# Encoder block on one Trainium2 core: five conv input pairs as Strassen products among the gate pairs, depthwise taps of four blocks on ScalarE and GpSimd

## The chip, the cores and the metric

One core of a Trainium2 chip runs the whole kernel in one launch. The metric is device time in microseconds. TensorE (PE) multiplies matrices, VectorE (DVE), ScalarE (ACT) and GpSimd (POOL) work on tiles, SyncE (SP) issues most of the loads. SBUF is the memory on the chip, PSUM the accumulators of TensorE.

## The reference

One residual layer over 512 tokens of 2048 features in float32. Cut to what this change touches:

```python
u = rms_norm(h, mix_pre_g)
proj = u @ w_in          # q, k, v, conv_a, conv_b (1024 each), gate_attn, gate_conv (2048 each)
y_attn = neighbourhood_attention(q, k, v, rpb) @ w_attn_o
z = ca * sigmoid(cb)                       # GLU
z = depthwise_conv(z, w_dw, width 31) + b_dw   # along the 512 tokens, each channel by itself
y_conv = silu(layer_norm(z)) @ w_conv_o
merged = sigmoid(ga) * y_attn + sigmoid(gb) * y_conv
h = h + rms_norm(merged @ w_out)
h = h + rms_norm((silu(gate) * up) @ w_down)   # gate, up = rms_norm(h) @ w_gate_up
```

## The kernel before

Features lie on the 128 partitions, the 512 tokens along a row, so that each output tile is 128x512. Float32 products are made of two halves: a weight tile is cast to `hi` on ACT (fp32r) and `lo = w - hi` is made on DVE; the activations are split likewise. A plain product is hi*lo + hi*hi + lo*hi, three matmuls of 512 columns for each of 16 blocks of 128 features (`gemm`, L178; `wchunk`, L137, loads, casts and subtracts one chunk of 8 blocks).

A pair of output blocks can instead be made by one Strassen product (Winograd's form) of 2x2 blocks (`strassen`, L264): seven products of 8 blocks each, where each block takes one matmul of 512 columns with the high half of the weights and one of 256 columns with the low half. Its moving operands (`op`, 56 tiles) are differences of parts of the normalised input. Each Strassen has seven casts of 128x1024 weights on ACT and seven subtractions on DVE (`halved_weights`, L250), three sums of weights on DVE (`wsum`, L274; the lines named by the profile are those of the calls and of L276 and L332), a weight sum S1 made by an accumulating DMA that POOL issues (`sums`, L237), three additions on DVE of a PSUM product and a copied tile (L317, L324, L330), and four joins of 256 columns (`joined`, L342).

The order of the work in the part that the change touches:

1. Input: the pairs 0 and 1 of conv_a and conv_b together with the load of x, with inputs that aren't yet normalised; their outputs are multiplied by the row factor `r1` in `conv`.
2. Plain conv pairs 2 to 7 (L493): for each, `gemm` of `cb` and of `ca`, then `conv` (L420), which makes z = ca * sigmoid(cb), starts the tile `cv` with the middle tap and the bias, and puts the other 30 taps on the list `todo`. During the last pair two chunks of x are loaded again and normalised (`normalize`, L484).
3. V (L504) in two halves, with the normalisation of the other chunks in the first.
4. Q, K and the attention, head by head (L596).
5. The first two gate pairs plainly, beside the making of the Strassen operands (L633).
6. Gate pairs 2 to 15 by Strassen (L692), each output through a sigmoid on ACT and stored to `g_d`. The layer norm's sum over channels (`csum`) is multiplied by ones behind the last one.
7. The attention's output product, the conv's layer norm and output product, the output projection, and the SwiGLU part, which is again mostly Strassen products.

The taps are DVE instructions `a += w * z` on shifted rows (`taps`, L440, instruction at L446). Every `wchunk` issues `rate` of them from the list: 4 a chunk in the conv stage, 3 and 4 in the halves of V, 4 in Q and K. `tc.keep_in_program_order` pins an instruction to its place in the program; the rest is put in order on each engine by a planner from its own costs and priorities. `issued_behind` (L102) only orders, it makes no engine wait.

On the memory: 66 slots of 128x512 hold most tiles; 56 of them are the Strassen operands in the gate stage. PSUM has eight banks in two pools, from which Strassens take three tiles in turn.

Of the kernel before, what the change touches and what calls it, by code (L numbers as in the profile page):

```python
# [31 lines left out]
P = 128  # L32
# [27 lines left out]
LN_AT = 5  # L60
R_CONV, R_V, R_QK = 4, (3, 4), 4
TAIL = 200
# [13 lines left out]
def hybrid_block(ctx: ExitStack, tc, xT, vecs, rpb, mask, w_c0, w_qk, w_v, w_gg, w_cg, w_ao, w_co, w_out, w_g0, w_gu, w_dn, outT):  # L76
# [54 lines left out]

    todo, rate = [], 0

# [130 lines left out]
    def strassen(w0, w1, op, name, n, s1=None, behind_last=None, first=None, quarters=None, apart=False, turn=True, midway=None):  # L264
# [19 lines left out]
        def product(ps, w, b, first=False, last=False, lo_first=False):  # L284
            hi, lo = w if isinstance(w, tuple) else halved_weights(w, name)
            ws = [slice(k * P, (k + 1) * P) for k in range(HT)]
            steps = [(hi, slice(0, NT)), (lo, A)]
            if lo_first:
                steps.reverse()
            for n, (wt, cols) in enumerate(steps):  # L290
                for k, t in enumerate(op[b]):
                    nc.tensor.matmul(
                        ps[:, cols], wt[:, ws[k]], t[:, cols], start=first and n + k == 0,
                        stop=last and n + k == HT, skip_group_check=True,
                    )

        def done(ps, i):
# [122 lines left out]
    def conv(i, pa, pb):  # L420
        sg = slot(f"sg{i}")
        nc.vector.tensor_tensor(out=sg, in0=pb, in1=r1, op=ALU.mult)
        nc.scalar.activation(sg, sg, AF.Sigmoid)
        nc.gpsimd.tensor_tensor(out=sg, in0=sg, in1=r1, op=ALU.mult)
        z = slot(f"z{i}")
        nc.vector.tensor_tensor(
            out=z.rearrange("p (r b c) -> p b r c", r=ROWS, b=2 * NB),
            in0=pa.rearrange("p (b r c) -> p b r c", r=ROWS, b=2 * NB),
            in1=sg.rearrange("p (b r c) -> p b r c", r=ROWS, b=2 * NB),
            op=ALU.mult,  # L430
        )
        a = slot(f"cv{i}")
        nc.vector.tensor_scalar(
            out=a, in0=z, scalar1=col(C_WDW, i * CW + PAD), scalar2=col(C_BDW, i), op0=ALU.mult, op1=ALU.add
        )
        for w in range(CW):
            if w != PAD:
                todo.append((i, z, a, w))

    def taps(n):  # L440

        for i, z, a, w in todo[:n]:
            to = slice(max(0, PAD - w), NT - max(0, w - PAD))
            fr = slice(max(0, w - PAD), NT - max(0, PAD - w))
            tc.keep_in_program_order(
# [4 lines left out]
            if w == CW - 1:  # L450
                if i == 0:
                    nc.gpsimd.tensor_copy(csum, a)
                else:
                    nc.gpsimd.tensor_tensor(out=csum, in0=csum, in1=a, op=ALU.add)  # L454
                nc.gpsimd.dma_start(c_d[i], a)
        del todo[:n]
# [35 lines left out]
    rate = R_CONV  # L492
    for i in range(2, CT):  # L493
        if i == CT - 1:
            for c in range(UN_EARLY):
                normalize(c)
        pb, pa = abank(f"cb{i}"), abank(f"ca{i}")
        gemm([(pb, w_cg[CT + i])], u, f"cb{i}", between=() if i > 2 else (first_convs,))
        gemm([(pa, w_cg[i])], u, f"ca{i}")
        conv(i, pa, pb)  # L500
# [106 lines left out]
    sm_ctx.close()  # L607
    stp = ctx.enter_context(tc.tile_pool(name="stp", bufs=2))
    g_d = dr.tile([2 * KT, P, NT], F32, name="g_d")

# [22 lines left out]
    for c in range(HT):  # L633
# [15 lines left out]
        if c >= G2_AT:  # L649
            quarters += [  # L650
                quarter(w_cg[2 * CT + KT * n + 2], h, "g2", load_in_order) for n, h in ((0, 0), (0, 1), (1, 0), (1, 1))[
                    2 * (c - G2_AT) : 2 * (c - G2_AT) + 2
# [13 lines left out]

    first = (quarters[0], *halved_weights(quarters[0], "g2", pin=True))
    s1 = stp.tile([P, 1024], F32, tag="S1", name="g2s1")
    tc.keep_in_program_order(nc.vector.tensor_tensor(out=s1, in0=quarters[2], in1=quarters[3], op=ALU.add))
# [21 lines left out]
    op = operands(b11, b2, t12, t34)  # L691
    for i in range(2, KT):  # L692
        if i > 2:
            s1, quarters = sums(w_cg[2 * CT + KT + 3], "g3", load_in_order) if i == 3 else None, None
        c11, c12, c21, c22 = strassen(
            w_cg[2 * CT + i], w_cg[2 * CT + KT + i], op, f"g{i}", i + 1, s1, quarters=quarters,
            first=first if i == 2 else None, apart=i == 2, midway=plain_gates if i == 2 else None,
        )
        if i == KT - 1:
# [6 lines left out]
            ya = [load_ya(h) for h in range(YA_EARLY)]  # L706

            pmu = abank("pmu")
            nc.tensor.matmul(pmu, ones, csum, start=True, stop=True)
            mu = slot("mu")  # L710
            nc.scalar.mul(mu, pmu, 1.0 / CONV)
        ga, gb = slot(f"ga{i}"), slot(f"gb{i}")
        joined(ga[:, A], c11)
        joined(ga[:, B], c12)
        nc.scalar.activation(ga, ga, AF.Sigmoid)
        nc.scalar.dma_start(g_d[i], ga)
        joined(gb[:, B], c22)
        joined(gb[:, A], c21)
        nc.scalar.activation(gb, gb, AF.Sigmoid)
        nc.scalar.dma_start(g_d[KT + i], gb)  # L720

# [262 lines left out]

    row = [const.tile([P, NT], F32, name=f"row{n}") for n in range(2)]

# [401 lines left out]
```

## Time and profile before

| | |
|---|---|
| median of 3 runs | 2485.11 us (2484.12 to 2485.39) |
| profiled execution | 2485.7 us, of which the span of instructions is 2483.9 us |
| mean granted TensorE clock | 0.997 |
| DVE busy | 2073.4 us (83%) |
| ACT busy | 1245.3 us (50%) |
| POOL busy | 492.9 us (20%) |
| plain conv pairs 2 to 7 | 51 to 183 us |
| V | 183 to 271 us |
| Q, K and attention | 271 to about 490 us |
| gate pairs 2 to 15 by Strassen | 524 to 799 us |

Times of instructions are counted from the start of the span. Rows of a timeline give the start, the duration, the engine, the line, the operation, output<-inputs by the program's names with shapes, and in brackets the idle time before it and what ended that. Durations include a start and an end that overlap with the neighbours', so their sum is a little above the busy time.

### The profile page before, as it was taken

Reading aid. Unit: us, or ns where it says so; the run is one execution under the profiler, and the core shown is the slowest. Engines: PE = TensorE matmul, PEld = TensorE weight load, DVE = VectorE, ACT = ScalarE, POOL = GpSimd, SP = SyncE. Lnnn points to the kernel's source line nnn. Section 1 sums busy time; section 2 is a strip of 40 time slices with the busy share of each in tenths; the row PEclk is TensorE's granted clock in tenths of the full one; section 3 lists DMA queues with packets and bytes.
Section 4 is the critical chain, followed back from the end, with each engine's and each line's share of the span. In section 5 each row is a group of like instructions: output and inputs, shape, how many; then the busy total and the mean of one; then the engine's idle time right before and its main releaser. Section 6 shows DMA issues by size and latency. Waiting matters only on the chain. (4 is left out here: it accounts for less than half of the span.)

```text
span 2483.9 us, 35789 instructions
## 1 busy us (share of the span) xinstructions
PE 2462.1 (99%) x13303; PEld 2131.3 (86%) x13303; DVE 2073.4 (83%) x2741; ACT 1245.3 (50%) x1932; POOL 492.9 (20%) x586
## 2 busy tenths in 40 slices
PE   9999999999999999999999999999999999999997
PEld 7888888888888888889888888888888888888887
DVE  5999887497777668878998888889898889989887
ACT  5223333365555434556555555555555565456553
POOL 0110242220000000021111112122222203532342
PEclk9999999999999999999999999999999999999998
DMA  6246332486667544669466666667666778889986
GB/s 215 90 144 203 103 106 95 135 265 194 190 187 230 186 144 136 204 214 301 138 179 182 174 169 174 184 196 215 206 193 201 216 237 235 239 228 254 223 219 202
DMA packets 165054, 472.33 MB, mean 190 GB/s; under 512 B 18768, under 2 KB 30928, under 8 KB 164880
## 3 DMA queue, kind: packets, MB, share of 16 engines
q1 hardware_dynamic: 109728, 334.02, 40.8%
q0 software_dynamic: 33168, 98.32, 18.7%
q10 hardware_dynamic: 21984, 37.72, 4.1%
q8 instruction: 104, 1.70, 0.3%
q14 instruction: 70, 0.57, 0.1%
HBM read 396.06 MB, written 71.30 MB: 188 GB/s over the span
## 5 line engine op out<-in xcount | busy, mean ns | idle before, releaser
L446 DVE SCALAR_TENSOR_TENSOR cv<-z,vec,cv 128x497 f32<-128x497 f32 (+14 forms) x240 | 188.3, 786 | 4.8
L996 POOL TENSOR_TENSOR row<-row,asq 128x512 f32<-128x512 f32 x30 | 55.5, 1851 | 405.4 <-ACT asq L995 405.4
L1153 POOL TENSOR_TENSOR ys<-ys,row 128x512 f32<-128x512 f32 x32 | 57.6, 1799 | 118.7 <-DVE ys L343 100.7
L147 ACT CAST whi_qk<-raw_qk 128x1024 fp32r<-128x1024 f32 x32 | 33.7, 1054 | 79.2 <-PE qk L196 62.6
L152 DVE TENSOR_TENSOR wlo_qk<-raw_qk,whi_qk 128x1024 fp32r<-128x1024 f32 x32 | 40.5, 1264 | 37.8 <-ACT whi_qk L147 37.7
L1020 POOL TENSOR_TENSOR an<-an,row 128x512 f32<-128x512 f32 x32 | 51.4, 1607 | 72.4 <-DMA an<-a_d 45.9
L147 ACT CAST whi_y<-raw_y 128x1024 fp32r<-128x1024 f32 x31 | 32.6, 1052 | 63.0 <-PE py L196 55.2
L531 POOL TENSOR_TENSOR bm<-braw,msk 128x64 f32<-128x64 f32 x96 | 53.7, 594 | 15.1 <-DMA braw<-in_rpb 15.0
L765 DVE TENSOR_TENSOR gg<-py,gg 128x512 f32<-128x512 f32 x32 | 21.8, 687 | 40.0 <-PE py L197 36.5
L193 PE MATMUL py<-ycl,whi_y 128*128 128x512 f32 x128 | 49.8, 389 | 0.0
L196 PE MATMUL py<-ych,whi_y 128*128 128x512 f32 x128 | 49.8, 389 | 0.0
L197 PE MATMUL py<-ych,wlo_y 128*128 128x512 f32 x128 | 49.8, 389 | 0.0
L152 DVE TENSOR_TENSOR wlo_y<-raw_y,whi_y 128x1024 fp32r<-128x1024 f32 x31 | 37.8, 1224 | 14.0 <-ACT whi_y L147 8.6
L454 POOL TENSOR_TENSOR csum<-csum,cv 128x512 f32<-128x512 f32 x7 | 12.7, 1814 | 141.4 <-DVE cv L446 141.4
L147 ACT CAST whi_ca<-raw_ca 128x1024 fp32r<-128x1024 f32 x12 | 12.6, 1054 | 46.3 <-PE cb L196 18.1
L568 ACT ACTIVATE sc<-sc,st 128x256 f32<-128x256 f32 x32 | 16.1, 505 | 30.8 <-DVE st L567 30.8
L796 POOL DMA_DIRECT2D m_d<-m x8 | 4.5, 556 | 135.7 <-ACT m L174 73.2
L1154 POOL DMA_DIRECT2D y_d<-ys x32 | 29.4, 918 | 9.3 <-POOL ys L1153 7.8
L147 ACT CAST whi_v<-raw_v 128x1024 fp32r<-128x1024 f32 x16 | 16.8, 1050 | 24.1 <-PE pv L519 17.5
L1083 DVE TENSOR_TENSOR sg<-sg,su 128x512 f32<-128x512 f32 x39 | 28.9, 740 | 0.0
L193 PEld LDWEIGHTS py<-ycl,whi_y 128*128 128x128 f32 x128 | 24.0, 188 | 5.0
L197 PEld LDWEIGHTS py<-ych,wlo_y 128*128 128x128 f32 x128 | 24.0, 188 | 5.0
(3343 smaller groups left out, 8718.4 us busy)
## 6 DMA issues: line engine op xcount, KB each, us to landing
raw_qk<-in_w_qk SPq DMA_DIRECT2D x32, 512.0 KB, 3.5
raw_w<-in_w_dn SPq DMA_DIRECT2D x24, 512.0 KB, 5.5
a_d<-sg ACTq DMA_DIRECT2D x41, 256.0 KB, 4.0
raw_v<-in_w_v SPq DMA_DIRECT2D x16, 512.0 KB, 4.4
gg<-g_d SPq DMA_DIRECT2D x32, 256.0 KB, 4.2
raw_y<-in_w_co SPq DMA_DIRECT2D x16, 512.0 KB, 3.7
raw_f<-in_w_g SPq DMA_DIRECT2D x16, 512.0 KB, 3.9
an<-a_d POOLq DMA_DIRECT2D x32, 256.0 KB, 5.8
```

The source lines that it names most:

```text
L147: ins = cast(hi[:, s], raw[:, s])
L152: nc.vector.tensor_tensor(out=lo[:, s], in0=raw[:, s], in1=hi[:, s].bitcast(F32), op=ALU.subtract)
L193: mmul = nc.tensor.matmul(ps, hi[:, s], al, start=first, stop=False)
L196: nc.tensor.matmul(ps, hi[:, s], ah, start=False, stop=False)
L197: nc.tensor.matmul(ps, lo[:, s], ah, start=False, stop=last)
L446: nc.vector.scalar_tensor_tensor(out=a[:, to], in0=z[:, fr], scalar=col(C_WDW, i * CW + w), in1=a[:, to], op0=ALU.mult, op1=ALU.add)
L531: nc.gpsimd.tensor_tensor(out=bm[:, o + i - i0], in0=raw[:, :, min(max(i, 0), 3) * EC : (min(max(i, 0), 3) + 1) * EC], in1=msk[:, o + i - ...
L996: nc.gpsimd.tensor_tensor(out=row[n], in0=row[n], in1=sq, op=ALU.add)
L1020: ins = nc.gpsimd.dma_start(t, a_d[DN_P + k]), nc.gpsimd.tensor_tensor(out=t, in0=t, in1=row[k // KT], op=ALU.mult)
L1083: nc.vector.tensor_tensor(out=t, in0=t, in1=up, op=ALU.mult)
L1153: tc.keep_in_program_order(nc.gpsimd.tensor_tensor(out=t, in0=t, in1=row[n], op=ALU.mult))
L1154: tc.keep_in_program_order(nc.gpsimd.dma_start(y_d[0, o], t, accum_op=ALU.add))
```

## The change

The plain conv stage ends after pair 2 (`PLAIN = 3`). The pairs 3 to 7 are made by `strassen` in the gate loop, which now has 19 rounds: rounds 0, 1, 4, 8 and 12 are the conv pairs 3, 4, 5, 6 and 7, with the weights of `cb` and `ca` in place of two gates, and the normalised input, so that the factor `r1` and the operations with it fall away for them. The GLU and the start of the taps become a function `glu`. Round 0, whose weights are loaded in the stage before and which has the plain gates' sigmoids in it, is now conv pair 3 in place of gate pair 2.

The taps of block 4 go on the list `todo`; two are issued on DVE behind each round. The taps of blocks 3, 5, 6 and 7 go on a list `pooled`: each `product` of a Strassen takes one from it, multiplies the shifted z by the tap's weight on ACT into a tile `tap` (two buffers) and adds that to `cv` on POOL. In ACT's order the multiplication stands behind the third matmul of the product. In the stages before, the taps of blocks 0, 1 and 2 are issued at two a chunk. The two chunks that are normalised early are so in pair 2, between `cb` and `ca`. The two rows that the SwiGLU part accumulates in get a pool of their own, opened where they are first used, so that the tap tiles' memory is free by then.

```diff
--- before.py
+++ after.py
@@ -58,7 +58,10 @@
 DN_3 = DN_2 + DN_P
 
 LN_AT = 5
-R_CONV, R_V, R_QK = 4, (3, 4), 4
+R_CONV, R_V, R_QK = 2, (2, 2), 2
+PLAIN = 3
+TAP_K = 2
+CONVS = {0: 3, 1: 4, 4: 5, 8: 6, 12: 7}
 TAIL = 200
 WARM = 17
 C0_PARTS = (0, 256), (256, 512), (512, 1024)
@@ -129,7 +132,7 @@
             behind.remove(eng)
             tc.keep_in_program_order(ins)
 
-    todo, rate = [], 0
+    todo, pooled, rate = [], [], 0
 
     def wraw(name):
         return wp.tile([P, 1024], F32, tag="raw", name=f"raw_{name}", bufs=5)
@@ -289,10 +292,12 @@
                 steps.reverse()
             for n, (wt, cols) in enumerate(steps):
                 for k, t in enumerate(op[b]):
-                    nc.tensor.matmul(
+                    mmul = nc.tensor.matmul(
                         ps[:, cols], wt[:, ws[k]], t[:, cols], start=first and n + k == 0,
                         stop=last and n + k == HT, skip_group_check=True,
                     )
+                    if (n, k) == (0, TAP_K):
+                        pooled_taps(1, mmul)
 
         def done(ps, i):
             t = stp.tile([P, HN], F32, tag="half", name=f"{name}c{i}", bufs=2)
@@ -422,6 +427,9 @@
         nc.vector.tensor_tensor(out=sg, in0=pb, in1=r1, op=ALU.mult)
         nc.scalar.activation(sg, sg, AF.Sigmoid)
         nc.gpsimd.tensor_tensor(out=sg, in0=sg, in1=r1, op=ALU.mult)
+        glu(i, pa, sg, todo)
+
+    def glu(i, pa, sg, queue):
         z = slot(f"z{i}")
         nc.vector.tensor_tensor(
             out=z.rearrange("p (r b c) -> p b r c", r=ROWS, b=2 * NB),
@@ -435,24 +443,43 @@
         )
         for w in range(CW):
             if w != PAD:
-                todo.append((i, z, a, w))
+                queue.append((i, z, a, w))
+
+    def shifted(w):
+        return slice(max(0, PAD - w), NT - max(0, w - PAD)), slice(max(0, w - PAD), NT - max(0, PAD - w))
+
+    def finished(i, a):
+
+        if i == 0:
+            nc.gpsimd.tensor_copy(csum, a)
+        else:
+            nc.gpsimd.tensor_tensor(out=csum, in0=csum, in1=a, op=ALU.add)
+        nc.gpsimd.dma_start(c_d[i], a)
+
+    def pooled_taps(n, behind=None):
+
+        for i, z, a, w in pooled[:n]:
+            to, fr = shifted(w)
+            t = tp.tile([P, NT], F32, tag="tap", name=f"tap{i}_{w}")
+            ins = nc.scalar.activation(t[:, to], z[:, fr], AF.Copy, scale=col(C_WDW, i * CW + w))
+            if behind:
+                issued_behind(ins, behind)
+            nc.gpsimd.tensor_tensor(out=a[:, to], in0=a[:, to], in1=t[:, to], op=ALU.add)
+            if w == CW - 1:
+                finished(i, a)
+        del pooled[:n]
 
     def taps(n):
 
         for i, z, a, w in todo[:n]:
-            to = slice(max(0, PAD - w), NT - max(0, w - PAD))
-            fr = slice(max(0, w - PAD), NT - max(0, PAD - w))
+            to, fr = shifted(w)
             tc.keep_in_program_order(
                 nc.vector.scalar_tensor_tensor(
                     out=a[:, to], in0=z[:, fr], scalar=col(C_WDW, i * CW + w), in1=a[:, to], op0=ALU.mult, op1=ALU.add
                 )
             )
             if w == CW - 1:
-                if i == 0:
-                    nc.gpsimd.tensor_copy(csum, a)
-                else:
-                    nc.gpsimd.tensor_tensor(out=csum, in0=csum, in1=a, op=ALU.add)
-                nc.gpsimd.dma_start(c_d[i], a)
+                finished(i, a)
         del todo[:n]
 
     u, acc = [], None
@@ -490,12 +517,12 @@
             un.append(split(t2, f"un{k}"))
 
     rate = R_CONV
-    for i in range(2, CT):
-        if i == CT - 1:
+    for i in range(2, PLAIN):
+        pb, pa = abank(f"cb{i}"), abank(f"ca{i}")
+        gemm([(pb, w_cg[CT + i])], u, f"cb{i}", between=() if i > 2 else (first_convs,))
+        if i == PLAIN - 1:
             for c in range(UN_EARLY):
                 normalize(c)
-        pb, pa = abank(f"cb{i}"), abank(f"ca{i}")
-        gemm([(pb, w_cg[CT + i])], u, f"cb{i}", between=() if i > 2 else (first_convs,))
         gemm([(pa, w_cg[i])], u, f"ca{i}")
         conv(i, pa, pb)
 
@@ -606,6 +633,8 @@
 
     sm_ctx.close()
     stp = ctx.enter_context(tc.tile_pool(name="stp", bufs=2))
+    tp_ctx = ExitStack()
+    tp = tp_ctx.enter_context(tc.tile_pool(name="tp", bufs=2))
     g_d = dr.tile([2 * KT, P, NT], F32, name="g_d")
 
 
@@ -648,7 +677,7 @@
 
         if c >= G2_AT:
             quarters += [
-                quarter(w_cg[2 * CT + KT * n + 2], h, "g2", load_in_order) for n, h in ((0, 0), (0, 1), (1, 0), (1, 1))[
+                quarter(w_cg[(1 - n) * CT + PLAIN], h, "k0", load_in_order) for n, h in ((0, 0), (0, 1), (1, 0), (1, 1))[
                     2 * (c - G2_AT) : 2 * (c - G2_AT) + 2
                 ]
             ]
@@ -664,8 +693,8 @@
         for rows, name, (ta, tb) in ((t12, "t12", ts[:2]), (t34, "t34", ts[2:])):
             rows.append([merged(ta, f"{name}{c}_0"), merged(tb, f"{name}{c}_1")])
 
-    first = (quarters[0], *halved_weights(quarters[0], "g2", pin=True))
-    s1 = stp.tile([P, 1024], F32, tag="S1", name="g2s1")
+    first = (quarters[0], *halved_weights(quarters[0], "k0", pin=True))
+    s1 = stp.tile([P, 1024], F32, tag="S1", name="k0s1")
     tc.keep_in_program_order(nc.vector.tensor_tensor(out=s1, in0=quarters[2], in1=quarters[3], op=ALU.add))
 
     def plain_gates():
@@ -689,12 +718,16 @@
         return split(ar[h], f"ya{h}")
 
     op = operands(b11, b2, t12, t34)
-    for i in range(2, KT):
-        if i > 2:
-            s1, quarters = sums(w_cg[2 * CT + KT + 3], "g3", load_in_order) if i == 3 else None, None
+    gates = iter(range(2, KT))
+    for n in range(CT - PLAIN + KT - 2):
+        conv_i = CONVS.get(n)
+        i = next(gates) if conv_i is None else conv_i
+        w0, w1 = (CT + i, i) if conv_i else (2 * CT + i, 2 * CT + KT + i)
+        if n:
+            s1, quarters = sums(w_cg[w1], f"g{n}", load_in_order) if n == 1 else None, None
         c11, c12, c21, c22 = strassen(
-            w_cg[2 * CT + i], w_cg[2 * CT + KT + i], op, f"g{i}", i + 1, s1, quarters=quarters,
-            first=first if i == 2 else None, apart=i == 2, midway=plain_gates if i == 2 else None,
+            w_cg[w0], w_cg[w1], op, f"g{n}", n + 1, s1, quarters=quarters,
+            first=None if n else first, apart=n == 0, midway=None if n else plain_gates,
         )
         if i == KT - 1:
 
@@ -705,19 +738,26 @@
                 load_ar()
             ya = [load_ya(h) for h in range(YA_EARLY)]
 
+            taps(len(todo))
+            pooled_taps(len(pooled))
             pmu = abank("pmu")
             nc.tensor.matmul(pmu, ones, csum, start=True, stop=True)
             mu = slot("mu")
             nc.scalar.mul(mu, pmu, 1.0 / CONV)
-        ga, gb = slot(f"ga{i}"), slot(f"gb{i}")
+        ga, gb = slot(f"ga{n}"), slot(f"gb{n}")
         joined(ga[:, A], c11)
         joined(ga[:, B], c12)
         nc.scalar.activation(ga, ga, AF.Sigmoid)
-        nc.scalar.dma_start(g_d[i], ga)
         joined(gb[:, B], c22)
         joined(gb[:, A], c21)
-        nc.scalar.activation(gb, gb, AF.Sigmoid)
-        nc.scalar.dma_start(g_d[KT + i], gb)
+        if conv_i:
+            glu(i, gb, ga, todo if n == 1 else pooled)
+        else:
+            nc.scalar.dma_start(g_d[i], ga)
+            nc.scalar.activation(gb, gb, AF.Sigmoid)
+            nc.scalar.dma_start(g_d[KT + i], gb)
+        taps(2)
+    tp_ctx.close()
 
 
     def layer_norm():
@@ -982,7 +1022,8 @@
         if c + 2 < HT:
             prepare(c + 2)
 
-    row = [const.tile([P, NT], F32, name=f"row{n}") for n in range(2)]
+    rw = ctx.enter_context(tc.tile_pool(name="rw", bufs=1))
+    row = [rw.tile([P, NT], F32, name=f"row{n}") for n in range(2)]
 
     def activated(j, t):
 
```

## The prediction

> **What bounds the kernel now.** I read the page's busy line first, then the engines' busy time by stretch, then TensorE's own waits, and last the timelines of VectorE (DVE) and GpSimd (POOL).
>
> ```profile
> PE 2462.1 (99%) x13303; PEld 2131.3 (86%) x13303; DVE 2073.4 (83%) x2741; ACT 1245.3 (50%) x1932; POOL 492.9 (20%) x586
> ```
>
> TensorE is busy throughout: a step that makes its instruction stream shorter is worth just what it takes off, as long as nothing else in that stretch becomes longer than the stream. So each stretch has to be looked at alone. The columns below are: stretch, its length, then busy us (and instructions) of PE, PEld, DVE, ACT, POOL.
>
> ```profile
> 74.30:183.10 108.80, 108.80 (x482) 90.09 (x481) 106.64 (x132) 26.37 (x30) 16.87 (x11) 1.00 0.39 124
> ...
> 661.70:681.20 19.50, 19.50 (x114) 17.20 (x113) 15.28 (x18) 10.78 (x16) 0.87 (x1) 1.00 0.64 189
> 1282.30:1301.80 19.50, 19.50 (x114) 17.20 (x113) 16.27 (x19) 10.92 (x15) 3.21 (x2) 1.00 0.61 181
> 1301.80:1321.30 19.50, 19.50 (x113) 17.21 (x112) 16.08 (x19) 10.92 (x15) 3.21 (x2) 1.00 0.60 169
> 1705.00:1724.50 19.50, 19.50 (x114) 17.21 (x113) 17.24 (x19) 10.81 (x16) 4.81 (x5) 1.00 0.69 203
> 1724.50:1744.00 19.50, 19.50 (x114) 17.20 (x113) 18.48 (x19) 10.80 (x16) 4.67 (x5) 1.00 0.69 203
> ```
>
> The first row is the five plain conv pairs 3 to 7: DVE is 98% busy there, with the taps, yet TensorE has no gap. The second is one Strassen of the gate stage: DVE 15.28 of 19.50, ACT 10.78, POOL 0.87. The last four are Strassens of the SwiGLU stage, the same products with one POOL add each (rows three and four) or two (five and six). I come back to their DVE column, which decides this case. Between 40 and 524 us TensorE waits almost for nothing; the largest wait is
>
> ```profile
> PE pv L519 <- DVE un15l L161: 0.4, 1, 0.4
> ```
>
> **The change, part by part.**
>
> *The products.* The plain pairs run from the end of pair 2 to the first matmul of V; a gate Strassen's length comes from the first matmul of the fourth and of the tenth.
>
> ```profile
> 74.04 0.39 PE L197 MATMUL ca<-u15h,wlo_ca 128*128 128x512 f32 x1
> ...
> 183.06 0.39 PE L517 MATMUL pv<-whi_v,un0h 128*128 128x512 f32 x1
> ```
> ```profile
> L292 PE MATMUL g<-b,g3h x24: 389/389/398, 544.9 to 561.4; 128*128 128x512 f32 x24
> ```
> ```profile
> L292 PE MATMUL g<-b,g9h x24: 389/389/398, 662.0 to 678.5; 128*128 128x512 f32 x24
> ```
>
> 183.06 - 74.27 = 108.8 us for five pairs, 21.76 each. (662.0 - 544.9) / 6 = 19.5 us for a Strassen. Five pairs moved: 5 x 19.5 - 108.8 = **-11.3 us**. That is the whole gain on TensorE; the change has to keep the gate stage at 19.5 us a Strassen to have it.
>
> *V and QK.* V loses its 0.4 us wait, since DVE does 2 taps a chunk where it did 3: **-0.4**. QK goes on as it is: it waits for nothing now. But V now starts at about 74 instead of 183 us, soon after the normalisation factor exists:
>
> ```profile
> 58.11 0.59 ACT L477 COPY r<-r_b 128x512 f32<-128x512 f32 x1
> ```
> ```profile
> L488 DVE SCALAR_TENSOR_TENSOR un<-xn,vec,r x16: 742/744/750, 163.5 to 221.3; 128x512 f32<-128x512 f32 x16
> ...
> L161 DVE TENSOR_TENSOR un0l<-un,un0h x1: 690/690/690, 166.0 to 166.0; 128x512 fp32r<-128x512 f32 x1
> ```
> ```profile
> L446 DVE SCALAR_TENSOR_TENSOR cv<-z,vec,cv x240: 720/743/1779, 63.8 to 406.1; 128x497 f32<-128x497 f32 x8, 128x499 f32<-128x499 f32 x8, 128x501 f32<-128x501 f32 x8, 128x503 f32<-128x503 f32 x8
> L433 DVE TENSOR_SCALAR cv<-z,vec x8: 535/546/550, 62.8 to 186.3; 128x512 f32<-128x512 f32 x8
> ...
> L454 POOL TENSOR_TENSOR csum<-csum,cv x7: 1292/1635/3382, 132.6 to 407.0; 128x512 f32<-128x512 f32 x7
> ```
>
> From 58.7 to 74.3 DVE has 15.6 us for two conv starts (2 x (0.69 + 0.69 + 0.55) = 3.9), three low weight halves of 1.22 (3.7), the first two normalised tiles (2 x 1.43 = 2.9) and six taps (4.5): 15.0, and the queue of x reloads beside it. That is tight: **+1**, ends 0 (it fits, as it did at 183 us) and +4 (two more tiles late).
>
> *Taps of block 4 on DVE.* Two for each Strassen, 2 x 0.743, about 1.45 us of DVE back to back, in fifteen of them.
>
> *Taps of blocks 3, 5, 6, 7.* 120, seven for each Strassen from the second (n = 1) to the eighteenth (n = 17). The ACT half is a copy with a scale of a 128x512 tile; the nearest row is the sigmoid:
>
> ```profile
> L715 ACT ACTIVATE ga<-ga x14: 625/625/633, 543.5 to 800.9; 128x512 f32<-128x512 f32 x14
> ```
>
> 7 x 0.63 = 4.4 us: ACT goes from 10.78 to 15.2 of 19.5. It has room, and costs nothing by itself; but the tap tile has two buffers, so ACT, in order, can be only two products ahead of POOL's adds, and behind a blocked tap product stand the casts of the weights that TensorE needs. POOL's adds therefore can't fall behind for good: seven must be done in each Strassen. The POOL half is 1.29 us alone (the minimum of L454): 9.0 us, with the 0.9 us issue of the weight sum 9.9 of 19.5. POOL as such has room as well; the weight sum that it issues is for a Strassen two further on, so a late issue harms nobody.
>
> *What the adds do to DVE* is the term that decides. Two pieces of the SwiGLU stage:
>
> ```profile
> 1706.69 1.29 POOL L996 TENSOR_TENSOR row<-row,asq 128x512 f32<-128x512 f32 x1 [13.19 <-ACT asq L995]
> 1706.74 2.32 DVE L276 TENSOR_TENSOR f29s<-f29s,f29q 128x1024 f32<-128x1024 f32 x1
> ...
> 1710.18 1.77 POOL L1020 TENSOR_TENSOR an<-an,row 128x512 f32<-128x512 f32 x1
> ...
> 1711.27 1.76 DVE L254 TENSOR_TENSOR f28l<-f28s,f28h 128x1024 fp32r<-128x1024 f32 x1 [0.47 <-ACT f28h L254]
> ```
> ```profile
> 1295.12 1.22 DVE L276 TENSOR_TENSOR f8s<-f8s,f8q 128x1024 f32<-128x1024 f32 x1
> 1296.47 0.70 DVE L317 TENSOR_TENSOR f<-f,f7v 128x512 f32<-128x512 f32 x1
> 1297.08 1.50 DVE L254 TENSOR_TENSOR f7l<-f7q,f7h 128x1024 fp32r<-128x1024 f32 x1
> ```
> ```profile
> 1295.15 2.35 POOL L996 TENSOR_TENSOR row<-row,asq 128x512 f32<-128x512 f32 x1 [15.83 <-ACT asq L995]
> ```
>
> An L276 that starts 0.05 us behind a POOL add takes 2.32 instead of 1.22: it stands still for 1.10. An add that starts 0.03 behind an L276 takes 2.35 instead of 1.29. So a POOL add and a DVE operation with both inputs in SBUF exclude each other, while L317, one of whose inputs is in PSUM, runs its usual 0.70 right through the add. In the Trainium skill, page "SBUF — State Buffer", section "Who interferes with whom", this is a rule: DVE's second SBUF input and GpSimd's reads go through one shared port pair, which one of them holds for its whole instruction; the traced 1.10 agrees.
>
> In a gate Strassen the operations with two SBUF inputs are seven low halves (L254), three weight sums (L276, L332) and one join: about 12.6 of DVE's 15.3 us.
>
> ```profile
> 662.00 1.23 DVE L332 TENSOR_TENSOR g9s<-g9q,g9s 128x1024 f32<-128x1024 f32 x1
> ...
> 663.14 1.22 DVE L254 TENSOR_TENSOR g9l<-g9s,g9h 128x1024 fp32r<-128x1024 f32 x1
> ...
> 666.59 1.11 PE L292 MATMUL g<-t,g9l 128*128 128x256 f32 x8
> ...
> 677.71 0.42 DVE L343 TENSOR_TENSOR gb<-g9v 128x256 f32<-128x256 f32 x1
> ```
>
> The port then has to carry 12.6 + 1.45 + 7 x 1.1 = 21.8 us of work in 19.5, or about 20.5 if the starts of operations (some 0.1 us each) lie outside the lock. DVE's own account: 15.28 + 1.45 + 7c, where c is what one add makes DVE lose beyond PSUM operations and idle gaps. The stretches give c. With the SwiGLU product (0.68) a Strassen without adds would be 15.96. One add: 16.27 and 16.08, so c is 0.31 and 0.12. Two adds: 17.24 and 18.48, so 0.64 and 1.26 each. The six adds average 0.70; the ends are 0.2 and 1.1. I take 0.65, below that mean, since an add that is late finds the PSUM operations, and well above the one-add rows, since at seven adds and two taps DVE has no idle left to hide them in. Then DVE needs 16.73 + 4.55 = 21.3 us a Strassen, which becomes the stage's length: +1.8 in fifteen of them, **+27**; in the two with adds but no taps 19.83, **+0.7**. The five conv outputs add a product (0.69) and a start of the taps (0.55) on DVE, 1.24 each, which have no cover any more: **+6.2** (0 if the cover stays). What is saved once is DVE's lead: the low half above was ready at 664.36 and used at 666.59, so the first **-2.2** of lateness is not felt.
>
> Sum: -11.3 - 0.4 + 1 + 27 + 0.7 + 6.2 - 2.2 = **+21 us** on the profiled execution's 2485.7, thus 2506.7; the median of the runs lies 0.6 below that, so **2506**.
>
> **The rivals.**
>
> *A, hidden after all (faster).* c stays where the one-add stretches have it, up to 0.31: 16.73 + 2.2 = 18.9 is below 19.5, lateness is made up in each Strassen, and the gain of 11.3 + 0.4 comes through: 2473.5, with +1 at the start of V 2474.5. For it: DVE loses little where adds fall on L317, and seven adds go out one to a product, as the three PSUM operations come at the ends of products. Against: 20.5 to 21.8 us of port work. The point where it decides is c = 0.46: 15 x (16.73 + 7 x 0.46 - 19.5) + 6.2 - 2.2 is the gain.
>
> *B, a draw.* c between 0.41 and 0.51, or A with V late by 4 and conv starts uncovered: 2480 to 2490.
>
> *C, no add finds cover.* Each costs the full 1.10: 16.73 + 7.7 = 24.4, +4.9 x 15 + 3.5 x 2 + 4 - 10.7 = +74, 2559. For it: the 1.26 of one two-add stretch. Against: TensorE would then wait, and DVE with it, and idle DVE is cover. Half way to it, at c = 0.85, DVE needs 22.7: +3.2 x 15 + 1.7 x 2 + 4 - 10.7 = +44, about 2529. The rule of the page named above, taken strictly with whole instructions (12.6 + 1.45 + 9.0 = 23.1 us a Strassen), would end near 2536.
>
> **How the numbers follow.** The stretched gate stage (c from 0.5 to 0.9) gets 0.53, A 0.32, B 0.09, C 0.06. Half of the stretched cases lie above 2506, few above 2529. The range takes in A's end, 2472, and goes to 2529; the likeliest case's own range is 2490 to 2529. About 0.2% (5 us) is what the measurement can tell from no change: faster 0.33, same 0.09, slower 0.58.
>
> **What would show it.** In the changed kernel's gate stage: Strassens longer than 19.5 us, about 21.3, from the second to the seventeenth, and 19.5 again for the last; DVE 95% busy or more; L254 well above 1.22 in the mean; the new POOL adds well above 1.29; TensorE waiting for the low halves on DVE. If Strassens stay at 19.5 us, the term of the adds is wrong and A is right. If V's first chunk shows TensorE waiting for the un tiles, the start was priced too low. If ACT's casts wait for the tap tile, the coupling through the two buffers is the worse one, and the time goes towards C.

## The result: 1.9% slower

The changed kernel takes 2531.89 us (median) against 2484.61: the ratio is 1.0186, 95% interval 1.0174 to 1.0199. The profiled execution took 2532.83 us, 47.1 more than the one before. The page's first lines of the changed kernel:

```profile
span 2531.0 us, 36379 instructions
...
PE 2468.9 (98%) x13383; PEld 2135.6 (84%) x13383; DVE 2120.5 (84%) x2681; ACT 1340.3 (53%) x2097; POOL 678.7 (27%) x706
...
L467 POOL TENSOR_TENSOR cv<-cv,tap 128x497 f32<-128x497 f32 (+14 forms) x120 | 209.3, 1744 | 139.9 <-ACT tap L464 137.3
...
L477 DVE SCALAR_TENSOR_TENSOR cv<-z,vec,cv 128x497 f32<-128x497 f32 (+14 forms) x120 | 103.6, 863 | 1.1
```

TensorE has less to multiply, yet its busy time is up by 6.8 us (matmuls at a lower clock, below) and it is idle for longer. The adds on GpSimd take 1.74 us in the mean instead of 1.29 alone; the VectorE taps 0.86 instead of 0.79, and 1.23 within the gate stage. VectorE's low halves there (L257, 128x1024) take 1.64 us in the mean, where they took 1.22 before.

Where the 47.1 us are, from the first matmuls of each stage in both traces: plain pairs 3 to 7 away, -108.8; V 4.8 longer (92.5 against 87.7); the Strassens 150.8 longer for five more rounds, of which 97.6 is five times 19.5 and 53.2 is stretch, the time by which the rounds are longer than that; the rest together +0.4 (V starts 1.9 us later, what follows the gate stage is 1.9 us shorter, and 0.4 lies between). The rounds of the gate stage in the changed kernel, one row each (columns as before: length, then busy us of PE, PEld, DVE, ACT, POOL, and the granted clock behind them):

```profile
443.00:463.10 20.10, 19.85 (x115) 17.36 (x114) 19.73 (x20) 13.81 (x21) 11.52 (x8) 1.00 0.69 204
463.10:488.50 25.40, 21.17 (x114) 18.51 (x114) 23.75 (x22) 14.66 (x23) 13.34 (x9) 0.93 0.44 139
...
581.60:603.20 21.60, 20.07 (x115) 17.41 (x115) 21.57 (x21) 14.76 (x22) 13.21 (x9) 1.00 0.59 170
603.20:624.90 21.70, 19.92 (x114) 17.25 (x113) 21.67 (x20) 14.71 (x22) 13.28 (x9) 1.00 0.59 171
624.90:650.80 25.90, 21.45 (x115) 18.46 (x114) 24.38 (x24) 15.03 (x23) 15.30 (x11) 0.93 0.54 166
650.80:670.90 20.10, 19.81 (x114) 17.29 (x113) 20.09 (x18) 13.94 (x21) 12.68 (x9) 1.00 0.48 144
```

DVE, at 15.28 of 19.50 before, is busy for the whole of an ordinary round of 20 to 22 us: it has become the bound. The four rounds behind a conv output (2, 5, 9 and 13, behind rounds 1, 4, 8 and 12) take 25 to 27 us, and round 4 takes 24.9, with a wait of 2.2 us at L329. TensorE's waits from V to the end of the gate stage name what it lacks (waited for: us in total, times, the longest); after these, it waits 1.1 to 1.4 us for a low half in each of seven rounds:

```profile
PE g L295 <- DVE g L329: 8.6, 13, 2.2
PE g L295 <- ACT g5v L284: 4.9, 1, 4.9
PE g L295 <- ACT g13v L284: 4.6, 1, 4.6
PE g L295 <- ACT g9v L284: 4.4, 1, 4.4
PE g L295 <- ACT g2v L284: 4.2, 1, 4.2
PE pv L544 <- ACT un4h L164: 2.4, 1, 2.4
```

Round 9 as an example, first DVE, then ACT and TensorE:

```profile
630.57 1.75 DVE L434 TENSOR_TENSOR z<-gb,ga 128x512 f32<-128x512 f32 x1
632.24 1.21 DVE L257 TENSOR_TENSOR g9l<-g9s,g9h 128x1024 fp32r<-128x1024 f32 x1
633.38 0.54 DVE L441 TENSOR_SCALAR cv<-z,vec 128x512 f32<-128x512 f32 x1
633.83 0.74 DVE L477 SCALAR_TENSOR_TENSOR cv<-z,vec,cv 128x511 f32<-128x511 f32 x1
634.49 1.21 DVE L279 TENSOR_TENSOR g10s<-g10s,g10q 128x1024 f32<-128x1024 f32 x1
635.63 1.72 DVE L477 SCALAR_TENSOR_TENSOR cv<-z,vec,cv 128x511 f32<-128x511 f32 x1
637.27 0.69 DVE L322 TENSOR_TENSOR g<-g,g9v 128x512 f32<-128x512 f32 x1
```
```profile
637.99 1.07 ACT L284 COPY g9v<-g 128x512 f32<-128x512 f32 x2 [4.37 <-DVE g L322]
638.63 1.53 PE L295 MATMUL g<-t,g9l 128*128 128x256 f32 x8 [4.45 <-ACT g9v L284]
...
639.96 3.29 PE L295 MATMUL g<-t,g9h 128*128 128x512 f32 x8
```

The addition L322 stands in DVE's order behind the GLU product, a low half, the start of the taps, two taps and a weight sum. ACT waits 4.37 us for it, and TensorE for ACT's copy, before it may write that bank again; the tap products wait in ACT's queue behind the copy, so GpSimd stands as well.

### The profile page after: what moved, and what is told of

It reads as the page before. It is cut to its first block, busy times and chain, and to the rows that moved or that the text cites. A ratio compares the mean times of both kernels' runs of the same rounds, so it can differ in the third digit from the quotient of the medians.

```text
span 2531.0 us, 36379 instructions
## 1 busy us (share of the span) xinstructions
PE 2468.9 (98%) x13383; PEld 2135.6 (84%) x13383; DVE 2120.5 (84%) x2681; ACT 1340.3 (53%) x2097; POOL 678.7 (27%) x706
## 5 line engine op out<-in xcount | busy, mean ns | idle before, releaser
L467 POOL TENSOR_TENSOR cv<-cv,tap 128x497 f32<-128x497 f32 (+14 forms) x120 | 209.3, 1744 | 139.9 <-ACT tap L464 137.3
L477 DVE SCALAR_TENSOR_TENSOR cv<-z,vec,cv 128x497 f32<-128x497 f32 (+14 forms) x120 | 103.6, 863 | 1.1
L464 ACT ACTIVATE tap<-z,vec 128x497 f32<-128x497 f32 (+14 forms) x120 | 85.6, 717 | 1.5 <-POOL cv L467 1.3
L558 POOL TENSOR_TENSOR bm<-braw,msk 128x64 f32<-128x64 f32 x96 | 41.7, 469 | 39.8 <-DMA braw<-in_rpb 39.8
L805 DVE TENSOR_TENSOR gg<-py,gg 128x512 f32<-128x512 f32 x32 | 21.8, 687 | 36.4 <-PE py L200 33.4
L368 POOL TENSOR_TENSOR r_r<-r_v,mhalf 128x2 f32<-128x2 f32 (+1 forms) x6 | 7.0, 1174 | 92.7 <-ACT whi_ca L150 52.4
L155 DVE TENSOR_TENSOR wlo_v<-raw_v,whi_v 128x1024 fp32r<-128x1024 f32 x16 | 19.6, 1224 | 14.4 <-ACT whi_v L150 14.2
L150 ACT CAST whi_v<-raw_v 128x1024 fp32r<-128x1024 f32 x16 | 16.8, 1051 | 24.3 <-PE pv L546 20.4
```

Of the source, the lines that this page charges most:

```text
L150: ins = cast(hi[:, s], raw[:, s])
L155: nc.vector.tensor_tensor(out=lo[:, s], in0=raw[:, s], in1=hi[:, s].bitcast(F32), op=ALU.subtract)
L464: ins = nc.scalar.activation(t[:, to], z[:, fr], AF.Copy, scale=col(C_WDW, i * CW + w))
L467: nc.gpsimd.tensor_tensor(out=a[:, to], in0=a[:, to], in1=t[:, to], op=ALU.add)
L477: nc.vector.scalar_tensor_tensor(out=a[:, to], in0=z[:, fr], scalar=col(C_WDW, i * CW + w), in1=a[:, to], op0=ALU.mult, op1=ALU.add)
L558: nc.gpsimd.tensor_tensor(out=bm[:, o + i - i0], in0=raw[:, :, min(max(i, 0), 3) * EC : (min(max(i, 0), 3) + 1) * EC], in1=msk[:, o + i - ...
```

## The experiments

Two theories stood against each other, with a third in one run. Exclusion: an add on GpSimd and a VectorE operation with two SBUF inputs keep each other out. Order on ScalarE: the tap products and their buffers delay what TensorE needs. VectorE's own load: the two taps and the conv starts are too much by themselves. The kernels of the first six experiments were each timed once (the kernel before took 2483.4 to 2484.2 us beside them), those with fewer pairs eleven times.

**No adds.** In `pooled_taps`:

```diff
-            nc.gpsimd.tensor_tensor(out=a[:, to], in0=a[:, to], in1=t[:, to], op=ALU.add)
```

> Leaves out the 120 adds on GpSimd (the conv sums of blocks 3, 5, 6, 7 lack 30 taps each); the 120 products on ScalarE stay. Exclusion (theory: an add on GpSimd and a VectorE operation with two SBUF inputs keep each other out): the rounds of the gate stage go from 22.5 us in the mean back to about 19.7, the four rounds behind a conv round to under 21, the time to about 2482. Order on ScalarE (rival: the tap products delay the casts and copies that TensorE waits for): the rounds stay above 21 us and the time above 2510. VectorE's own load (rival: two taps and the conv starts are too much by themselves): the four rounds behind conv rounds stay at 24 to 25 us, the time about 2500.

Measured 2480.84 us. Rounds 1 to 17, in this kernel and in the changed one:

```profile
441.00:775.00 334.00, 333.02 (x1908) 292.67 (x1907) 281.40 (x331) 249.83 (x370) 28.07 (x27) 1.00 0.61 187
```
```profile
443.00:825.90 382.90, 347.17 (x1906) 301.29 (x1905) 370.92 (x328) 245.67 (x366) 226.25 (x143) 0.97 0.54 161
```

A round is 19.6 us without the adds, 22.5 with them; the four long ones are gone too (20.2 at most). ScalarE's products all run here and cost nothing. DVE is busy for 89.5 us less: 0.75 us for each of 120 adds, none of which is its own work. Its low halves take 1.23 us in the mean instead of 1.64. VectorE's load and the order on ScalarE are refuted as causes by themselves.

**Fills in place of the adds.** The same place:

```diff
-            nc.gpsimd.tensor_tensor(out=a[:, to], in0=a[:, to], in1=t[:, to], op=ALU.add)
+            for _ in range(2):
+                nc.gpsimd.memset(t, 0.0)
```

> Each of the 120 adds on GpSimd is replaced by two fills of the tap tile with zeros, which only write (the conv sums of four blocks lack 30 taps each). ScalarE's products, the two buffers and the waits between ScalarE and GpSimd stay. Exclusion by reading: VectorE's operations of 128x1024 keep 1.22 us, and the time is that of the kernel without adds, about 2482. Rival (any work on GpSimd holds VectorE up, or the coupling through the two tap buffers costs): VectorE's operations are lengthened again, and the time is 2510 or more if the fills take about as long as the adds did.

Measured 2480.19 us.

```profile
441.60:776.10 334.50, 332.75 (x1907) 292.45 (x1906) 282.37 (x329) 249.57 (x370) 149.38 (x265) 1.00 0.61 187
```
```profile
L468 POOL MEMSET tap<- x240: 517/527/886, 445.9 to 778.4; 128x512 f32 x120
...
L464 ACT ACTIVATE tap<-z,vec x120: 697/717/727, 445.1 to 777.0; 128x497 f32<-128x497 f32 x8, 128x498 f32<-128x498 f32 x8, 128x499 f32<-128x499 f32 x8, 128x500 f32<-128x500 f32 x8
```

Two fills are 1.05 us of GpSimd for each tap, with the same two buffers and the same waits for the tap tile, and DVE is as free as with none; its low halves take 1.23 us. A fill is shorter than an add and doesn't wait for the start of `cv`, so this run alone leaves that open; the run with DMAs below keeps the order on `cv` and agrees. What holds VectorE up is that GpSimd reads SBUF. The rule of the Trainium skill, page "SBUF — State Buffer", section "Who interferes with whom", has it so: such a VectorE operation contends with a GpSimd instruction that reads, not with one that only writes. The 282.37 against 370.92 us agree.

**No taps on VectorE in the rounds.** Block 4's list is dropped:

```diff
-        taps(2)
+        if todo:
+            finished(*todo[-1][::2])
+            todo.clear()
```

> Leaves out the 30 taps of block 4 on VectorE (its conv sum has the middle tap alone); the adds on GpSimd stay. By the account of the prediction (15.28 + 7 x 0.65 = 19.8 us a round) the ordinary rounds go from 21.1 to about 20, the four rounds behind conv rounds from 26 to about 23, the time to about 2500. If the port alone sets the length (12.6 + 7 x 1.1 = 20.3 us), ordinary rounds stay at 20.3 or above. Rival (the taps hardly matter, the adds do): 2522 or more.

Measured 2514.02 us. Seventeen rounds take 365.5 us, 21.5 each, not 20:

```profile
441.20:806.70 365.50, 341.31 (x1907) 296.37 (x1906) 341.12 (x297) 245.65 (x366) 222.34 (x143) 0.99 0.56 168
```

DVE is 29.8 us less busy, 0.99 for each tap of 0.74: the rest, which went with the taps, fits their waiting for GpSimd. VectorE's busy time is close to what the account said (341.12 us, 20.1 a round, against 19.8), but it is idle for 24 us now, twice as long as in the changed kernel, 11.0 of it at L322 until TensorE has finished a product. The account "VectorE's busy time is the length of the round" failed here.

**All taps on VectorE.** ScalarE's and GpSimd's part undone, the five Strassens kept:

```diff
-                        pooled_taps(1, mmul)
+                        taps(1)
...
-            glu(i, gb, ga, todo if n == 1 else pooled)
+            glu(i, gb, ga, todo)
```

> Undoes the ScalarE and GpSimd part alone: the taps of blocks 3, 5, 6, 7 are fused multiply-adds on VectorE as the others, one at each product, beside the two at the end of a round; five pairs stay Strassen products. Account: nine taps at 0.70 us make 15.28 + 6.3 = 21.6 us of VectorE a round, against 15.28 + 1.45 + 7c with the adds. If an add costs VectorE as much as a tap does (c about 0.7), the time is that of the changed kernel within 10 us: 2522 to 2542. If the adds cost more (c about 0.9 to 1.0): about 2510 or less. If they cost little and the long rounds come from elsewhere: 2550 or more.

Measured 2513.91 us, 18 us under the changed kernel.

```profile
440.80:809.00 368.20, 346.38 (x1906) 300.20 (x1905) 354.83 (x449) 178.25 (x250) 25.83 (x27) 0.97 0.55 167
```

DVE is 354.83 - 281.40 = 73.4 us busier than without those taps, 0.61 for each; the add on GpSimd cost it 0.75. Taking a tap off VectorE in this way gives it more work than the tap was. Five pairs are too many for VectorE by either way: 21.7 us a round, of which VectorE is idle for 0.8, without a single add.

**The GLU later.**

```diff
-CONVS = {0: 3, 1: 4, 4: 5, 8: 6, 12: 7}
+CONVS = {0: 3, 1: 4, 3: 5, 7: 6, 11: 7}
...
-            glu(i, gb, ga, todo if n == 1 else pooled)
+            with tc.high_priority(offset=-TAIL):
+                glu(i, gb, ga, todo if n == 1 else pooled)
...
-        taps(2)
+        taps(0 if conv_i else 2)
```

> All of the computation is kept. The GLU product and the start of the taps get a lower priority in the planner's order, no DVE tap follows a conv round, and conv rounds 4, 8, 12 become 3, 7, 11, so that ScalarE needs the new z later. Theory (the 4 to 5 us waits in the rounds behind conv rounds come from the GLU burst standing before the addition at L322 in VectorE's queue, which TensorE's next product into the same bank needs): these rounds go from 25 to 27 us to about 22, four times 4 us: about 2516, while ordinary rounds stay at 21. Rival (VectorE is simply full, and what it does later costs the same): the total stays within 5 us of 2531.

Measured 2539.68 us: neither the theory's 2516 nor the rival's 2531 within 5. The total doesn't decide between them, since the gate stage and what follows it went opposite ways. Rounds 1 to 17:

```profile
441.90:820.20 378.30, 347.14 (x1906) 300.94 (x1905) 370.62 (x322) 245.54 (x366) 222.26 (x141) 0.97 0.54 162
```

They take 4.6 us less than in the changed kernel, with VectorE as busy as there (370.62 against 370.92 us), but six of its taps come later now, four of them at the very end of the stage, and the last round is 1.7 us longer: 2.9 us are saved. The rounds behind conv rounds, now 2, 4, 8 and 12, take 22.0, 24.2, 21.0 and 25.6 us, and TensorE's longest wait for a copy at L284 falls from 4.9 to 3.2 us; but other rounds grow, up to 25.0. So this order saves some 3 of the 16 us that the theory gave it, which fits the rival: VectorE is simply full. The next stage starts 4.0 us earlier than in the changed kernel (at 844.0 against 848.0), and yet the end is 6.9 us later: 10.9 us are lost behind the gate stage, where TensorE waits 5.2 us more than there (for the sum over channels 1.6, since its taps come so late; for `h_sq` 1.7, for a copy at L284 1.9). Why the edit lengthened the rest isn't shown.

**V without taps in its first half.**

```diff
-R_CONV, R_V, R_QK = 2, (2, 2), 2
+R_CONV, R_V, R_QK = 2, (0, 2), 3
```

> All of the computation is kept. No tap is issued on VectorE in the first half of V (0 a chunk instead of 2), three instead of two a chunk in Q and K. Theory (V starts right behind the normalisation factor, and VectorE can't make the normalised tiles in time): V's length from its first to QK's first product goes from 92.5 to about 88.5 us, the wait for un4 and the slower matmuls behind it go, the time to about 2527. Rival (the reloads of x come too late): V stays at 92 us.

Measured 2525.68 us. V before and here:

```profile
76.10:168.60 92.50, 89.78 (x386) 72.28 (x386) 68.40 (x91) 29.40 (x38) 3.17 (x3) 0.98 0.57 187
```
```profile
74.50:161.80 87.30, 87.30 (x386) 72.06 (x385) 58.78 (x77) 29.63 (x38) 1.29 (x1) 1.00 0.57 195
```

The first is the changed kernel, the second this one. V's 5 us came from VectorE being late with the normalised tiles: with fewer taps there TensorE waits for none.

**Fewer pairs.** Two pairs (6, 7) and three pairs (5, 6, 7) by Strassen, with all taps on VectorE, one beside each of some products (a Strassen's seven are named "11", "T2", "T1", "T3", "21", "22", "T4"); for two:

```diff
-R_CONV, R_V, R_QK = 2, (2, 2), 2
-PLAIN = 3
+R_CONV, R_V, R_QK = 4, (1, 3), 3
+PLAIN = 6
-CONVS = {0: 3, 1: 4, 4: 5, 8: 6, 12: 7}
+CONVS = {0: 6, 1: 7}
...
-                        pooled_taps(1, mmul)
+                        taps(1 if b in ("11", "T2", "21", "T4") else 0)
...
-            glu(i, gb, ga, todo if n == 1 else pooled)
+            glu(i, gb, ga, todo)
-        taps(2)
+        taps(0)
```

> All of the computation is kept. Only pairs 6 and 7 are Strassen products (rounds 0 and 1 of 16); all taps are on VectorE, those of these two blocks four a round beside single products, none on ScalarE or GpSimd; taps before: 4 a chunk in the plain pairs, 1 and 3 in V, 3 in Q and K. Account: 2 x 2.25 us less on TensorE; VectorE 15.28 + 4 x 0.70 = 18.1 of 19.5 us a round, so the rounds stay at 19.5 but the one or two behind a GLU: 2481 to 2483, faster than before by 0.1%. Rival (single taps among the products delay the addition at L322 wherever they stand, as the GLU does): some rounds at 20 to 21 us, 2485 to 2500.

> All of the computation is kept. Pairs 5, 6 and 7 are Strassen products (rounds 0, 1 and 5 of 17), with five taps a round on VectorE and none on ScalarE or GpSimd. Account: 6.7 us less on TensorE; VectorE 15.28 + 5 x 0.70 = 18.8 of 19.5 us a round, with little left for the GLU: if the rounds stay at 19.5, about 2479; with one lost us in half of the rounds 2487. It tells from how full a VectorE the rounds begin to stretch.

Two pairs: 2479.56 us, 0.9980 of before (0.9971 to 0.9989): 4.6 us less, where TensorE's account gave 4.5. Three pairs (`PLAIN = 5`, `CONVS = {0: 5, 1: 6, 5: 7}`, "T1" in the list as well): 2482.85, 0.9996 (0.9987 to 1.0005). From the second on the rounds are 19.5 us in both (round 1 is 20.4 with three pairs), with DVE busy for 91% and 95% of the time:

```profile
519.90:773.60 253.70, 253.70 (x1459) 223.82 (x1458) 232.06 (x279) 140.70 (x197) 14.05 (x15) 1.00 0.61 189
```
```profile
499.10:772.30 273.20, 273.20 (x1571) 241.01 (x1570) 259.42 (x316) 151.38 (x212) 16.73 (x18) 1.00 0.62 191
```

Three pairs reach the next stage 1.8 us earlier, but the sum over channels is late there (the last ten taps ran behind each other) and 3.9 us are lost up to the end. So 1.3 us remain of the forecast 6.7. With a sixth tap in two rounds of three (`n_` counts the Strassens):

```diff
-                        taps(1 if b in ("11", "T2", "T1", "21", "T4") else 0)
+                        taps(1 if b != "22" and (b != "T3" or n_ % 3) else 0)
```

> All of the computation is kept. As the three pairs with five taps a round, but a sixth in two rounds of three, so that no taps are left over at the end of the gate stage. Theory (with five a round the last ten taps ran in one piece, the sum over channels came late, and the stage behind lost some 4 us): the wait for the sum (1.7 us) and the one for m (2.2 us) go, the rounds stay at 19.5 to 19.6: about 2478. Rival (at six taps VectorE is full, 15.28 + 6 x 0.61 = 18.9 us and no place for the GLU): rounds of 20 us and more, 2483 to 2490.

2480.76 us, 0.9983 (0.9974 to 0.9992): no different from two pairs, and 3.4 us of 6.7. The wait for the sum went, the one for m, the input of the output projection (2.2 us), stayed.

**Three pairs, block 5 the changed kernel's way, and by DMA.** Four taps a round on VectorE for blocks 6 and 7, block 5 through `pooled_taps` at "T3", "22" and, in place of a VectorE tap, none at "T1"; in the second, the add is

```diff
-            nc.gpsimd.tensor_tensor(out=a[:, to], in0=a[:, to], in1=t[:, to], op=ALU.add)
+            nc.gpsimd.dma_start(a[:, to], t[:, to], accum_op=ALU.add)
```

> All of the computation is kept. Three pairs; four taps a round on VectorE for blocks 6 and 7, and the 30 taps of block 5 as products on ScalarE and adds on GpSimd, at most two a round, the way of the changed kernel. VectorE's account: 15.28 + 4 x 0.61 + 2 x 0.75 = 19.2 us, about the same as with six taps on VectorE. If a GpSimd add costs VectorE as much as a tap also where VectorE isn't full, VectorE's busy time over the rounds is that of the kernel with five or six taps a round or above, and the time 2478 to 2484. If adds at two a round fall into idle gaps (0.31 and 0.12 us each, as with one add a round in the SwiGLU stage): VectorE some 10 us less busy over the stage, about 2477.

> All of the computation is kept. As the one before, but the 30 adds of block 5 are accumulating DMAs from tile to tile that GpSimd issues, so that GpSimd reads nothing itself. If only the reading excludes VectorE: VectorE's operations of 128x1024 keep 1.22 us, the rounds 19.5 us, the time about 2478. If an accumulating DMA takes 6 us from issue to landing and the next waits for it (4.1 to 7.3 us were traced before for such a DMA), two a round still fit; if ScalarE has to wait for the tap tile then, rounds of 20 us and more, above 2485.

2482.92 us (0.9992, 0.9983 to 1.0001) and 2482.76 us (0.9994, 0.9985 to 1.0003). The rounds are 19.5 us in both; first the adds, then the DMAs:

```profile
498.90:772.10 273.20, 273.20 (x1571) 241.00 (x1570) 266.09 (x300) 166.92 (x237) 59.58 (x46) 1.00 0.61 186
```
```profile
498.90:772.10 273.20, 273.20 (x1570) 241.00 (x1569) 251.06 (x303) 168.02 (x239) 40.28 (x45) 1.00 0.79 215
```

28 of the adds fall into this stretch and cost DVE 15.0 us more than the DMAs do, 0.54 each (a little more, since it finishes three instructions fewer here). They lengthen the weight sums (L279, 1.50 us in the mean against 1.22) and the joins (L348, 0.59 against 0.42), while the low halves keep 1.23. Here DVE is 97% busy as in the changed kernel, and the rounds still keep 19.5. So the adds are harmless as long as what they take from VectorE fits. The time isn't the 2478 us forecast for the DMAs, though VectorE's instructions and the rounds are as forecast: in round 16 TensorE waits 2.5 us for a copy at L284 and is slow behind it (eight matmuls take 3.46 us instead of 2.00), and it waits 2.2 us for m.

**Four pairs with DMAs** (`PLAIN = 4`, `CONVS = {0: 4, 1: 5, 5: 6, 10: 7}`, block 4 by DMA):

> All of the computation is kept. Pairs 4 to 7 as Strassen products (rounds 0, 1, 5, 10 of 18); the taps of blocks 5, 6, 7 on VectorE, five or six a round, those of block 4 as products on ScalarE and accumulating DMAs, at most two a round. TensorE has 2.25 us less than with three pairs. If VectorE bears 15.28 + 5.5 x 0.61 = 18.6 us a round with 1.24 more behind three conv rounds, the rounds stay near 19.6 and the time is about 2477, the lowest of all; if the GLU bursts lengthen three rounds by 2 us each, 2483, no better than two pairs.

2483.63 us, 0.9998 (0.9989 to 1.0007). Fifteen rounds at 19.5 to 19.6, then 20.4 and 23.8; 3.0 of the last are TensorE's waiting for the sum over channels, which stands behind the last taps. V takes 90.2 us here, 3 more than with three pairs. Two pairs with VectorE taps, or three with them spread evenly, are the versions whose gain over the kernel before is clear of the noise, 0.2%.

## Why the prediction was wrong, step by step

The profiled execution is 26 us above the forecast's +21: 4.2 of it in V, 21.5 in the gate stage, 0.4 elsewhere. The sign and the mechanism behind the adds were right.

- *Products, -11.3.* Right as a term: without the adds the rounds are back at 19.6 us. The kernel without adds gains 4.8 us and not 11.3 over the profile before, mainly since V takes 4.6 and the rounds, a little over 19.5, 2.4.
- *V, -0.4 + 1.* Too low: +4.8, just past the upper end given. The mechanism was the one named, tiles late from VectorE: 2.4 us of waiting for un4, and about as much again because the matmuls behind it were slow (below).
- *Adds exclude VectorE's two-input operations.* Right, and shown: adds out, or replaced by writes, and the stretch goes.
- *c = 0.65.* Measured 0.75 of busy time. VectorE's whole account for rounds 1 to 17 was right within 2%, in part by luck: 15.28 x 17 + 1.45 x 15 + 119 x 0.65 + 6.2 = 365 us against 370.92 measured, since its other work came to 281.4 instead of 287.7 and the adds to 89.5 instead of 77, which cancel by half.
- *"Then DVE needs 16.73 + 4.55 = 21.3 us a Strassen, which becomes the stage's length."* This is the step that failed most: it put VectorE's own idle time at nothing. The seventeen rounds take 382.9 us, 12 more than VectorE is busy. Of these 12, some 4 end with a product of TensorE and some 7 with a cast or copy of ScalarE: where TensorE stops for VectorE for 4 us, ScalarE stops behind it, TensorE comes back slowly, and VectorE in turn waits for both. The run without VectorE taps shows it again (24 us idle), and so does the one with all taps on VectorE and no adds (13 us).
- *The other sum, 12.6 + 1.45 + 7 x 1.1 = 21.8 us, or 23.1 with whole instructions*, which the forecast didn't use, lies on either side of the measured 22.5 us a round; without VectorE taps it is 20.3 to 21.6, against 21.5. By the timelines an add or a VectorE operation with two SBUF inputs was under way for 362 of the 382.9 us, and for 349 of the 365.5 without VectorE taps, but for 242 of 273.2 where three pairs with adds keep 19.5. So what the two engines can't do at once was itself nearly full. No run separates this from the idle time above; the run with all taps on VectorE only shows that such idle time also comes without adds.
- *The lead, -2.2.* It didn't show: before, L317 (now L322) waits for TensorE only, so the chain product, addition, copy, next product had no lead of that size, and the low halves' lead was beside the point. Stretch 53.2 against 31.7 forecast: 6 from VectorE's busy time, 12 from its idle time, 2.2 from the lead, about 2 from the last round (22.1 us up to the next stage, 20.0 before), all rounded.
- *What TensorE waits for.* The low halves were named; they cost it 8.4 us in seven rounds. As much is lost at the addition L329 (8.6), and twice as much at the copies behind L322 (18 in the four long rounds).
- *ScalarE blocked by the two tap buffers.* Didn't occur: 1.3 us in all.
- *Rival A, hidden* is refuted for seven adds a round; at two a round (with four VectorE taps) the rounds do hold. *Rival C* is where the time lies, by a smaller c and the idle time.

## What to carry to other kernels

Before work moves from VectorE to GpSimd, count what the GpSimd instruction reads: beside VectorE operations with two SBUF inputs, a 128x512 add took 0.54 to 0.75 us of VectorE's time here, while the fused tap that it replaced took 0.61. So this offloading gained VectorE next to nothing; fills, which only write, and accumulating DMAs took nothing from it that shows. And an engine's busy sum is a lower bound on the stage's length, not its length: at 97% busy the rounds once held at 19.5 us and once took 22.5.

## What the hardware showed that was not expected

TensorE's matmuls were slower after quite short waits. In V the wait for un4 was 2.4 us, and behind it:

```profile
89.58 0.64 PE L544 MATMUL pv<-whi_v,un4h 128*128 128x512 f32 x1 [2.40 <-ACT un4h L164]
90.02 0.63 PE L545 MATMUL pv<-wlo_v,un4h 128*128 128x512 f32 x1
```
```profile
89.60:93.00 3.40, 3.09 (x7) 1.98 (x8) 3.40 (x6) 1.49 (x2) 0.00 (x0) 0.53 0.76 224
93.00:97.00 4.00, 4.00 (x19) 3.28 (x18) 3.96 (x7) 0.62 (x1) 0.00 (x0) 0.98 0.86 284
```

The granted clock is 0.53 for the next 3.4 us, matmuls take 0.63 instead of 0.39 us, then it is full again. Round 9 above shows the same behind its 4.45 us: 3.29 us for eight matmuls that take 2.00. So a wait of 2.4 us cost nearly twice itself, and each of the four long rounds 1.3 to 2.6 us more than its wait. The Trainium skill, page "TensorE: Matmul & The Clock Gate", Part 1, has half speed after an idle window of about 3.4 us; here 2.4 us was enough. The length of the wait alone doesn't decide it: waits of 1.1 to 1.4 us in the changed kernel left the clock at 1.00 for the next 3.4 us, one of 2.20 us in round 4 brought it to 0.52, and with the GLU later a wait of 2.02 us brought it to 0.50, while one of 2.28 us left it at 1.00.

An accumulating DMA from tile to tile, issued by GpSimd (0.87 us each, 5.6 us to landing in the median), left VectorE's weight sums of 128x1024 (L279) at 1.22 us in the mean; beside as many adds they took 1.50.
